# A fifth pair of rows in each quarter of the down projection, with the plain additions ahead of the joining ones

## The chip, the cores and the metric

The kernel is one program on one core of a Trainium2 chip. The metric is the device time of one execution in microseconds (us); several executions are timed and their median is given. The core has a matrix engine (PE, with its weight loads listed as PEld), a vector engine (DVE), a scalar engine (ACT), GpSimd (POOL) and a queue for transfers (SP). Each engine works through its own list of instructions in the order in which the program holds them; semaphores tie the lists together. A matrix product is written into one of eight banks of PSUM, each 128 x 512 floats.

## The reference, cut to what matters

One layer of a hybrid decoder runs on 256 tokens of width 2048: attention in two forms, gates, an output projection, a feed-forward part (up, a causal convolution of width 3, gelu times value, down), and an embedding gate (pg). The change touches the feed-forward part, above all `down`:

```python
up = causal_depthwise_conv(u @ w_up[i], conv_w[i], conv_b[i])
gate_ff, value = jnp.split(up, [D_FF], axis=-1)          # D_FF = 5632
f = (jax.nn.gelu(gate_ff, approximate=True) * value) @ w_down[i]
h = h + rmsnorm(f, g_ffn_post[i])
```

All inputs are float32. A product is made from three matrix products of reduced operands: each factor x is split into a high part (rounded) and a low part (x minus the high part), and high x high, high x low and low x high are summed. "Three products" below means these.

## The kernel before, in words

**Rows and quarters.** The 5632 inner rows of `down` are 44 blocks of 128 ("rows" from here on), worked in four quarters of 11 rows (`NQ`, `QT`). A quarter first makes its 22 tiles of `up` (one per gate row and one per value row; `mm` at L382 and L384, then `up_evac`), and then multiplies its 11 rows with the 2048 columns of `w_down`, adding to the running sum `ff`. Of these columns, the first 1024 go through `strassen` and the last 1024 through two calls of `plain` (columns 1024 to 1535 and 1536 to 2047), which call `four`. In the first quarter (q = 0) `plain(2)` stands ahead of `strassen`; in the other three both plains stand behind it.

**Pairs and plain rows.** In `strassen` a pair of rows is a 2 x 2 block product (two halves of the tokens, two rows, two column groups of 512) made with seven products instead of eight: 7 x 3 = 21 matmuls of 128 x 512. A plain row takes 2 x 2 x 3 = 12, so two plain rows take 24. `DROWS = 8` gives four pairs and three plain rows (L1431: `range(DROWS, QT)`). A pair needs sums of four token blocks (`parts`, L1209 to L1212, split at L1215 and L1218 into `mixed`) and sums of weight blocks. Of the weight sums, the first two of a pair are made by transfers while `up` runs (`sum_early`: one load by SP, two adding transfers by POOL, into `tsum`); the next two are made by DVE from them (`wsum`, L257 and L258). `sum_early` is called at the places in `AHEAD` (L1394, L1401).

**Weights.** Weights come in items of 128 x 1024. SP loads an item into `raw` (five buffers, `NRAW`), ACT writes its high part (`hi`, L238 or L234), DVE its low part (`lo`, L301 or L295), into seven buffers (`NSPL`). A pair has four items (a row, two of sums, half a row), a plain row one, `plain(2)` five and a half. `tick` runs at the start of each item: it issues high parts ahead of their use, then the low parts (`lows`) of all items that had a high part before this tick, and the work handed over with `defer`. `lows` also issues the next loads; a `raw` buffer is loaded again when its low part is done.

**Where the sums go.** `strassen` takes eight banks: those of products 1, 5, 6 and 7, and one for each place (token half, column half) of the result, which collect products 2, 3, 4 and the plain rows. Product 1 is copied out by ACT (L1289). What is left for DVE is twelve additions of 128 x 512 in q > 0: eight in `join_to` (L1321 to L1328, from products 6, 7, 5) and four in `ends` (L1332, from the four places). Both are handed to `defer`, so they are issued in a later tick, behind that tick's low parts:

```python
bk = next(s)                                   # L1432, after the pairs
defer((None, ... join_to(o, bk, x)))           # L1434, q > 0
next(s)                                        # L1439, after the plain rows
defer((None, lambda bk=bk, o=o: ends(o, bk)))  # L1440
```

`plain(2)` then asks `bank()` for two banks (one for each token half); the pool gives banks whose last reader has been issued.

## Time and profile before

| what | value |
|---|---|
| median of 3 runs | 1431.91 us (1430.57 to 1432.77) |
| the profiled execution | 1429.95 us, of which 1428.2 us are the span of the profile |
| HBM traffic | 302.50 MB read, 215 GB/s over the span |
| DMA share of `up` of the second quarter (800 to 905 us) | 0.70 |
| DMA share of its `down` (911 to 967 us) | 0.66 |

The span runs from the first instruction to the last. A row of the timeline gives the start and length in us, the engine, the line, the operation, what it writes and reads, the shape, and how many equal instructions that follow each other were merged into it; in brackets stands how long the engine had been idle and what ended that. A matmul's end is modelled: the next one starts before it ends, so the distance from start to start says what a matmul takes.

### The profile page before, as it was taken

To read this page: it belongs to the slowest core of one execution; us is meant where nothing else is said; L and a number is where in the kernel's file an instruction comes from. 1 tells how busy PE (TensorE), PEld (TensorE's weight loads), DVE (VectorE), ACT (ScalarE), POOL (GpSimd) and SP (SyncE) were. 2 spreads that over 40 slices of the span, in tenths; PEclk is the share of its full clock that TensorE was granted. 3 is DMA by queue.
4 is the path that set the end of the run, shared out by engine and by line. 5 is a ranking of instruction groups with operands and counts; after the bars stand their busy time and mean duration, and the time that the engine had idled before them with its cause. 6 is when DMAs were issued, how large, how long until landed. Compare 5 with 4: busy or idle time off the path is not lost.

```text
span 1428.2 us, 20626 instructions
## 1 busy us (share of the span) xinstructions
PE 1421.1 (100%) x7511; PEld 1223.2 (86%) x7511; DVE 1156.9 (81%) x1777; ACT 858.1 (60%) x1296; POOL 53.4 (4%) x65
## 2 busy tenths in 40 slices
PE   9999999999999999999999999999999999999998
PEld 8888888888888888898888888888888888888787
DVE  7876666669889965689988788987889878898798
ACT  7665555566655655676666566645566455665564
POOL 0000000002110000000000000000000000000000
PEclk9999999999999999999999999999999999999999
DMA  7754746479985766558857785377853778538754
GB/s 290 268 169 157 246 145 220 149 235 254 300 230 198 268 217 221 192 175 267 253 168 245 243 264 179 109 271 233 263 183 111 266 229 266 187 113 321 210 177 162
DMA packets 93814, 309.10 MB, mean 216 GB/s; under 512 B 10256, under 2 KB 10896, under 8 KB 93456
## 3 DMA queue, kind: packets, MB, share of 16 engines
q1 hardware_dynamic: 85072, 292.05, 60.6%
q0 software_dynamic: 8640, 15.73, 6.4%
q8 instruction: 59, 0.97, 0.3%
q14 instruction: 43, 0.35, 0.1%
HBM read 302.50 MB, written 5.24 MB: 215 GB/s over the span
## 4 chain that ended last, share of the span: by engine, by line
PE 98%; DVE 1%; ACT 0%; issue 0%
PE mm L382 33%; PE mm L945 30%; PE mm L384 17%; PE mm L710 2%; PE mm L708 2%; PE mm L709 2%; PE mm L863 2%; PE mm L865 2%; PE mm L864 2%; PE S L382 0%; PE mm L404 0%; PE mm L403 0%; PE mm L402 0%; DVE lo L301 0%; PE S L721 0%; PE po L721 0%
## 5 line engine op out<-in xcount | busy, mean ns | idle before, releaser
L301 DVE TENSOR_TENSOR lo<-raw,hi 128x1024 fp32r<-128x1024 f32 (+1 forms) x498 | 581.3, 1185 | 115.0 <-ACT hi L238 110.2
L382 PE MATMUL mm<-u,hi 128*128 128x512 f32 x1804 | 627.4, 392 | 0.0
L238 ACT ACTIVATE hi<-raw 128x1024 fp32r<-128x1024 f32 (+1 forms) x498 | 504.1, 1026 | 189.9 <-PE mm L382 54.4
L384 PE MATMUL mm<-u,lo 128*128 128x256 f32 x1791 | 501.4, 280 | 0.0
L382 PEld LDWEIGHTS mm<-u,hi 128*128 128x128 f32 x1804 | 336.7, 187 | 72.4
L384 PEld LDWEIGHTS mm<-u,lo 128*128 128x128 f32 x1791 | 338.5, 189 | 0.6
L945 PE MATMUL mm<-hi,ft 128*128 128x512 f32 x544 | 173.4, 389 | 0.0
L945 PE MATMUL mm<-hi,u 128*128 128x512 f32 (+1 forms) x464 | 148.0, 389 | 0.6 <-DVE u L1503 0.5
L440 ACT ACTIVATE t<-mm 128x256 f32<-128x256 f32 x131 | 49.8, 380 | 149.3 <-PE mm L384 149.2
L945 PEld LDWEIGHTS mm<-hi,ft 128*128 128x128 f32 x544 | 102.1, 188 | 21.1
L945 PE MATMUL mm<-lo,ft 128*128 128x512 f32 x272 | 105.8, 389 | 0.0
L945 PEld LDWEIGHTS mm<-hi,u 128*128 128x128 f32 x464 | 86.4, 188 | 19.1 <-DVE u L1503 2.2
L443 DVE TENSOR_TENSOR s<-mm,t 128x256 f32<-128x256 f32 x116 | 49.0, 422 | 54.4 <-ACT t L440 54.4
L945 PE MATMUL mm<-lo,u 128*128 128x512 f32 (+1 forms) x232 | 89.6, 386 | 0.0
L382 PE MATMUL mm<-mg,hi 128*128 128x512 f32 x232 | 80.5, 392 | 0.0
L277 POOL DMA_DIRECT2D tsum<-in_w x36 | 31.7, 1017 | 886.4 <-DMA tsum<-in_w 269.1
L384 PE MATMUL mm<-mg,lo 128*128 128x256 f32 x230 | 64.4, 280 | 0.0
L234 ACT ACTIVATE hi<-wsum 128x512 fp32r<-128x512 f32 x68 | 41.2, 629 | 36.0 <-DVE wsum L257 27.1
L945 PEld LDWEIGHTS mm<-lo,ft 128*128 128x128 f32 x272 | 51.1, 188 | 10.5
L1232 ACT ACTIVATE cv<-cpad,cw 128x256 f32<-128x256 f32 x88 | 52.5, 596 | 11.7 <-DVE cpad L1227 11.6
L945 PE MATMUL mm<-hi,mixed 128*128 128x512 f32 x160 | 55.8, 389 | 0.0
L945 PEld LDWEIGHTS mm<-lo,u 128*128 128x128 f32 x232 | 43.6, 188 | 9.0 <-DVE lo L295 0.5
(327 smaller groups left out, 1871.2 us busy)
## 6 DMA issues: line engine op xcount, KB each, us to landing
raw<-in_w SPq DMA_DIRECT2D x470, 512.0 KB, 4.2
tsum<-in_w POOLq DMA_DIRECT2D x36, 256.0 KB, 6.9
raw<-in_w SPq DMA_DIRECT2D x32, 256.0 KB, 3.2
tsum<-in_w SPq DMA_DIRECT2D x13, 512.0 KB, 4.6
gh<-in_w SPq DMA_DIRECT2D x12, 512.0 KB, 5.9
gh<-in_w POOLq DMA_DIRECT2D x24, 256.0 KB, 7.7
hd<-in_head SPq DMA_DIRECT2D x6, 576.0 KB, 7.5
gh<-in_gx SPq DMA_DIRECT2D x6, 512.0 KB, 5.3
```

What stands on the lines that cost most here:

```text
L234: ACT.activation(hi[i][:, n * 512:(n + 1) * 512], x, AF.Copy)
L238: ACT.activation(hi[i][:, a:b], raw[i][:, a:b] if src is None else src, AF.Copy)
L277: nc.gpsimd.dma_start(x, w[stream[i] + 1 - NE][:, 512:], accum_op=OP.add)
L301: DVE.tensor_tensor(lo[i][:, a:b], raw[i][:, a:b] if src is None else src, f(hi[i][:, a:b]), OP.subtract)
L382: PE.matmul(ps, wh, rhs, start=first, stop=last, skip_group_check=True)
L384: PE.matmul(ps[:, :T], wl, rhs[:, :T], start=False, stop=last, skip_group_check=True)
L440: ACT.activation(t1[0], ps[:, T:], AF.Copy)
L443: DVE.tensor_tensor(out, ps[:, :T], t1[0], OP.add)
L708: PE.matmul(pv[t], xh, wh, start=kt == 0, stop=False)
L709: PE.matmul(pv[t], xh, wl, start=False, stop=False)
L945: PE.matmul(ps, x[i], w[j], start=first and n == 0, stop=last and n == 2, skip_group_check=True)
L1232: ACT.activation(y, c[:, 2:], AF.Identity, scale=cw[:, n, 2:3], bias=cw[:, n, 3:4])
```

## The change

The number of paired rows in a quarter of `down` goes from eight to ten: five pairs and one plain row. The fifth pair's mixed token sums get a tile of their own (`mixed4`, in the place of the `hx` tile with number 0), and its first two weight sums come by transfers in `up`, as those of the others do (`AHEAD` has a fifth place; the sum lies in the place of `hx` number 3). In q > 0, `ends` is now issued at once after the plain rows, and `join_to` after it, in two parts that `defer` hands to two ticks. In q = 0 the order is as it was.

```diff
 PAIRS = 4
-DROWS = 8
+DROWS = 10
 DSUM = {"down": DROWS // 2, "pg": 2}
...
-        tt(x2, bk[6], x, OP.add)
-        tt(o[0, 0], o[0, 0], x, OP.add)
-        tt(x, bk[7], x2, OP.add)
-        tt(x2, bk[5], x2, OP.subtract)
-        tt(o[1, 0], o[1, 0], x, OP.add)
-        tt(x, bk[5], x, OP.subtract)
-        tt(o[0, 1], o[0, 1], x2, OP.add)
-        tt(o[1, 1], o[1, 1], x, OP.add)
+
+        def banks_free():
+            tt(x2, bk[6], x, OP.add)
+            tt(o[0, 0], o[0, 0], x, OP.add)
+            tt(x, bk[7], x2, OP.add)
+            tt(x2, bk[5], x2, OP.subtract)
+
+        def rest():
+            tt(o[1, 0], o[1, 0], x, OP.add)
+            tt(x, bk[5], x, OP.subtract)
+            tt(o[0, 1], o[0, 1], x2, OP.add)
+            tt(o[1, 1], o[1, 1], x, OP.add)
+        defer((None, banks_free))
+        defer((None, rest))
...
         bk = next(s)
-        q == 0 and join_first(o, bk)
-        defer((None, (lambda bk=bk, o=o: join(o, bk)) if q == 0 else lambda bk=bk, o=o, x=x: join_to(o, bk, x)))
+        if q == 0:
+            join_first(o, bk)
+            defer((None, lambda bk=bk, o=o: join(o, bk)))
...
         next(s)
-        defer((None, lambda bk=bk, o=o: ends(o, bk)))
+        if q == 0:
+            defer((None, lambda bk=bk, o=o: ends(o, bk)))
+        else:
+            ends(o, bk)
+            join_to(o, bk, x)
```

What this does to the engines' lists shows best in the second quarter (q = 1); the third and fourth read alike.

**DVE, from the last pair's last item on, before.** `lo_9103` is the half row that ends the fourth pair, `lo_9116`, `lo_9128` and `lo_9137` are the three plain rows, and `lo_9150`, `lo_9162` and `lo_9174` the first three items of `plain(2)`; `mm_9026` is product 6.

```order
L301 TENSOR_TENSOR lo_9103<-raw_9001,hi_9102 128x512 [waits Activation_49]
L301 TENSOR_TENSOR lo_9116<-raw_9019,hi_9115 128x1024 [waits DMAHW7_49,Activation_49]
L301 TENSOR_TENSOR lo_9128<-raw_9059,hi_9127 128x1024 [waits DMAHW0_49,Activation_49]
L301 TENSOR_TENSOR lo_9137<-raw_9071,hi_9136 128x1024 [waits DMAHW1_49,Activation_49]
L301 TENSOR_TENSOR lo_9150<-raw_9107,hi_9149 128x1024 [waits DMAHW2_49,Activation_49]
L301 TENSOR_TENSOR lo_9162<-raw_9119,hi_9161 128x1024 [waits DMAHW3_49,Activation_49]
L301 TENSOR_TENSOR lo_9174<-raw_9131,hi_9173 128x1024 [waits DMAHW4_49,Activation_49]
L1321 TENSOR_TENSOR x2_9188<-mm_9026,x1_8971 128x512 [waits PE_49]
L1322 TENSOR_TENSOR ff_5993<-ff_5993,x1_8971 128x512
```

**The same place in the changed kernel.** `lo_9186` is the half row that ends the fifth pair, `lo_9199` the one plain row, `lo_9211` to `lo_9257` the first five items of `plain(2)`; `mm_9070`, `mm_9025`, `mm_9057` and `mm_9280` are the four places of the result, `mm_9025` that of the first token half and the second column group.

```order
L301 TENSOR_TENSOR lo_9186<-raw_9094,hi_9185 128x512 [waits Activation_49]
L301 TENSOR_TENSOR lo_9199<-raw_9106,hi_9198 128x1024 [waits DMAHW3_49,Activation_49]
L301 TENSOR_TENSOR lo_9211<-raw_9142,hi_9210 128x1024 [waits DMAHW4_49,Activation_49]
L301 TENSOR_TENSOR lo_9220<-raw_9154,hi_9219 128x1024 [waits DMAHW5_49,Activation_49]
L301 TENSOR_TENSOR lo_9233<-raw_9190,hi_9232 128x1024 [waits DMAHW6_49,Activation_49]
L301 TENSOR_TENSOR lo_9245<-raw_9202,hi_9244 128x1024 [waits DMAHW7_49,Activation_49]
L301 TENSOR_TENSOR lo_9257<-raw_9214,hi_9256 128x1024 [waits DMAHW0_49,Activation_49]
L1338 TENSOR_TENSOR ff_5993<-ff_5993,mm_9070 128x512 [waits PE_49]
L1338 TENSOR_TENSOR ff_5993<-ff_5993,mm_9025 128x512 [waits PE_49]
L1338 TENSOR_TENSOR ff_5993<-ff_5993,mm_9057 128x512 [waits PE_49]
L1338 TENSOR_TENSOR ff_5993<-ff_5993,mm_9280 128x512 [waits PE_49]
L301 TENSOR_TENSOR lo_9266<-raw_9223,hi_9265 128x1024 [waits DMAHW1_49,Activation_49]
```

The first addition stands behind six low parts of full items in both; what moved is that three of the six were plain rows before and one is now, that the additions are those of the four places, and that `join_to` (now L1323 to L1332) follows later.

**PE, from the last plain row into `plain(2)`, before.** `mm_9206` is a place of the result, `mm_9246` and `mm_9247` are the banks of `plain(2)` for the two token halves; in the built program `mm_9247` stands in bank 0, which `mm_9026` held.

```order
L945 MATMUL mm_9206<-hi_9136,ft_5994 128x512
L945 MATMUL mm_9206<-lo_9137,ft_5994 128x512
L945 MATMUL mm_9206<-hi_9136,ft_5994 128x512
L945 MATMUL mm_9246<-hi_9149,ft_5994 128x512 [waits Activation_49]
L945 MATMUL mm_9246<-lo_9150,ft_5994 128x512 [waits DVE_49]
L945 MATMUL mm_9246<-hi_9149,ft_5994 128x512
L945 MATMUL mm_9247<-hi_9149,ft_5994 128x512 [waits DVE_49]
L945 MATMUL mm_9247<-lo_9150,ft_5994 128x512
```

**The same place in the changed kernel.** `mm_9289` and `mm_9290` are the banks of `plain(2)`; `mm_9290` stands in bank 2, which `mm_9025` held.

```order
L945 MATMUL mm_9280<-hi_9198,ft_5994 128x512 [waits PE_49]
L945 MATMUL mm_9280<-lo_9199,ft_5994 128x512
L945 MATMUL mm_9280<-hi_9198,ft_5994 128x512
L945 MATMUL mm_9289<-hi_9210,ft_5994 128x512 [waits Activation_49]
L945 MATMUL mm_9289<-lo_9211,ft_5994 128x512 [waits DVE_49]
L945 MATMUL mm_9289<-hi_9210,ft_5994 128x512
L945 MATMUL mm_9290<-hi_9210,ft_5994 128x512 [waits DVE_49]
L945 MATMUL mm_9290<-lo_9211,ft_5994 128x512
```

The fourth matmul of `plain(2)` waited for the first addition of `join_to` (L1321, the last reader of `mm_9026`) and now waits for the second addition of `ends` (the last reader of `mm_9025`).

**DVE, near the end of `up` in the changed kernel.** `y4_8955` holds the fifth pair's token sums, `s_8960` is the sum of the next `up` tile, `lo_8949` the row item of the second pair.

```order
L483 TENSOR_TENSOR ft_5994<-cv0_8828,ft_5994 128x256 [waits Activation_49]
L1209 TENSOR_TENSOR y4_8955<-cv0_8709,cv0_8828 128x128
L1210 TENSOR_TENSOR y4_8955<-y4_8955,cv0_8709 128x128 [waits DVE_49]
L1211 TENSOR_TENSOR y4_8955<-cv0_8709 128x128
L1212 TENSOR_TENSOR y4_8955<-y4_8955,cv0_8828 128x128 [waits DVE_49]
L443 TENSOR_TENSOR s_8960<-mm_8884,t1_8946 128x256 [waits Activation_49]
L1227 TENSOR_TENSOR cpad_5995<-s_8960,R_76 128x256 [waits DVE_49]
L301 TENSOR_TENSOR lo_8949<-raw_8780,hi_8948 128x1024 [waits DMAHW3_49,Activation_49]
L1218 TENSOR_TENSOR mixed4_6181<-y4_8955,mixed4_6181 128x512 [waits Activation_49]
L1235 SCALAR_TENSOR_TENSOR cv0_8943<-cpad_5995,cw_77,cv0_8943 128x256 [waits Activation_49]
```

The five rows L1209 to L1212 and L1218 are new here; the others stood in the same order before.

## The prediction

> **What bounds the kernel now.** I read the page first (busy time, then the chain that ended last), then the waits of PE, then the busy time of each engine in the stretch of the second quarter's `down`.

> ```profile
> PE 1421.1 (100%) x7511; PEld 1223.2 (86%) x7511; DVE 1156.9 (81%) x1777; ACT 858.1 (60%) x1296; POOL 53.4 (4%) x65
> PE 98%; DVE 1%; ACT 0%; issue 0%
> PE z L594 <- DVE epsb L563: 1.1, 1, 1.1
> PE mm L945 <- DVE u L1503: 0.5, 2, 0.3
> PE mm L1492 <- DVE hx L1463: 0.3, 1, 0.3
> 911.00:967.00 56.00, 56.00 (x248) 46.37 (x247) 46.99 (x60) 31.57 (x39) 0.00 (x0) 1.00 0.66 223
> ```

> PE is the path: 98% of the chain, and its waits on other engines sum to 1.9 us, none of them in the four quarters. In the stretch from 911 to 967 us (second quarter's `down`; the columns are length, PE, PEld, DVE, ACT, POOL, granted clock, DMA share, GB/s) PE has no idle time and the clock is 1.00. So a matmul taken away is worth its full distance, and any new wait of PE costs its full length. DVE is second, 46.99 of 56 us there. The question is whether it stays second once the stage holds more of its work.

> **What is removed.** Two rows of PE's timeline, an item of twelve matmuls apart:

> ```profile
> 929.62 0.39 PE L945 MATMUL mm<-lo,ft 128*128 128x512 f32 x1
> 932.34 0.39 PE L945 MATMUL mm<-lo,ft 128*128 128x512 f32 x1
> 938.24 0.39 PE L945 MATMUL mm<-hi,ft 128*128 128x512 f32 x1
> ```

> 932.34 - 929.62 = 2.72 us for twelve, 0.227 us each. A quarter loses 24 matmuls and gains 21: 3 x 0.227 = 0.68 us, and four quarters save **2.72 us**. The third row is the first matmul of the second token half of `plain(2)`, the one that waits for a bank (found by asking for a window after the end of the matmul ahead). In the changed kernel PE would want to start it 0.68 us earlier, at 937.56.

> **What the fifth pair costs DVE.** DVE in the same quarter, from the third pair to the additions, with two rows of ACT and one of PE:

> ```profile
> 917.03 0.68 DVE L257 TENSOR_TENSOR wsum<-tsum,raw 128x512 f32<-128x512 f32 x1
> 922.51 0.68 DVE L257 TENSOR_TENSOR wsum<-tsum,raw 128x512 f32<-128x512 f32 x1
> 923.84 1.29 DVE L295 TENSOR_TENSOR lo<-tsum,hi 128x512 fp32r<-128x512 f32 x2
> 926.22 0.39 PE L945 MATMUL mm<-lo,mixed 128*128 128x512 f32 x1
> 926.25 5.22 DVE L301 TENSOR_TENSOR lo<-raw,hi 128x512 fp32r<-128x512 f32 x5
> 930.60 1.06 ACT L238 ACTIVATE hi<-raw 128x1024 fp32r<-128x1024 f32 x1 [1.22 <-DMA raw<-in_w]
> 931.70 1.23 DVE L301 TENSOR_TENSOR lo<-raw,hi 128x1024 fp32r<-128x1024 f32 x1 [0.23 <-ACT hi L238]
> 932.62 1.06 ACT L238 ACTIVATE hi<-raw 128x1024 fp32r<-128x1024 f32 x1 [0.96 <-DMA raw<-in_w]
> 933.71 1.23 DVE L301 TENSOR_TENSOR lo<-raw,hi 128x1024 fp32r<-128x1024 f32 x1 [0.79 <-ACT hi L238]
> 934.86 0.68 DVE L1321 TENSOR_TENSOR x<-mm,x 128x512 f32<-128x512 f32 x1
> 943.44 2.48 DVE L1332 TENSOR_TENSOR ff<-ff,mm 128x512 f32<-128x512 f32 x4
> DMA to landing us min/median/max: 3.5/4.5/4.8
> ```

> From the wsum of the third pair to that of the fourth DVE takes 922.51 - 917.03 = **5.48 us a pair** without idle time; PE takes 21 x 0.227 = 4.76. So DVE loses 0.72 us to PE in each pair. In the fourth pair it is still ahead: the low part of its first sums ends at 923.84 + 1.29 = 925.13, and PE reads it at 926.22, 1.1 us later. A fifth pair takes that to about 0.4.

> Behind the last pair's half row (the first of the five merged at 926.25) DVE does six low parts. The last two wait for ACT, and ACT for the transfer: the `raw` buffer of the sixth item is the one that the first of the six frees, at 926.25 + 0.60 + 1.22 = 928.1, and it lands 4.5 us later, at 932.6, which is the median of the view on `raw` for 926 to 940 us (last row). Only then, at **934.86**, comes the first addition. Now PE had three plain rows (8.16 us) to pass meanwhile, and the freed bank was there at 935.54, 2.7 us ahead of 938.24. In the changed kernel the same six low parts, with the same five buffers behind them, stand ahead of the first addition (the order above shows it), but PE passes one plain row, 2.72 us.

> **What else is put on DVE.** The fifth pair's token sums and their low part. The rows of the fourth pair, and the place where the fifth's will stand:

> ```profile
> 882.65 0.29 DVE L1209 TENSOR_TENSOR y<-cv,cv 128x128 f32<-128x128 f32 x1
> 883.58 0.42 DVE L443 TENSOR_TENSOR s<-mm,t 128x256 f32<-128x256 f32 x1
> 885.51 0.68 DVE L1218 TENSOR_TENSOR mixed<-y,mixed 128x512 fp32r<-128x512 f32 x1
> 886.12 0.48 DVE L1235 SCALAR_TENSOR_TENSOR cv<-cpad,cw,cv 128x256 f32<-128x256 f32 x1
> 903.88 0.42 DVE L483 TENSOR_TENSOR ft<-cv,ft 128x256 fp32r<-128x256 f32 x1
> 905.45 0.42 DVE L443 TENSOR_TENSOR s<-mm,t 128x256 f32<-128x256 f32 x1 [1.14 <-ACT t L440]
> ```

> The four sums take 883.58 - 882.65 = 0.93 us and fall into the 1.14 us for which DVE waits ahead of 905.45: nothing. The low part takes 886.12 - 885.51 = 0.61, call it **0.60**, and comes behind that wait; from there DVE's rows follow each other closely up to the additions (one wait of 0.49 at 915.89 hangs on DVE's own earlier result and moves along), so all of it arrives. Bounds: 0 if a wait takes it up, 0.77 if the sums spill over by the 0.17 us that they pushed L443 in the fourth pair's case.

> With it the fifth pair's sums come 1.1 - 0.72 - 0.60 = -0.2 us, that is 0.2 us late. This is no term of its own: PE would wait for the bank right after anyway.

> **The added wait.** First addition: 934.86 + 5.48 + 0.60 = 940.94. Four additions take 2.48 (last row but one above), so they start 0.60 apart and take 0.68: the second ends at 940.94 + 0.60 + 0.68 = 942.22. PE wants the bank at 937.56: a wait of **4.66 us**. The other two quarters with this order:

> ```profile
> 1114.27 0.68 DVE L1321 TENSOR_TENSOR x<-mm,x 128x512 f32<-128x512 f32 x1
> 1117.55 0.39 PE L945 MATMUL mm<-hi,ft 128*128 128x512 f32 x1
> 1293.82 0.68 DVE L1321 TENSOR_TENSOR x<-mm,x 128x512 f32<-128x512 f32 x1
> 1296.86 0.39 PE L945 MATMUL mm<-hi,ft 128*128 128x512 f32 x1
> ```

> Third: 1114.27 + 7.36 = 1121.63 against 1117.55 - 0.68 = 1116.87, 4.76 us. Fourth: 1293.82 + 7.36 = 1301.18 against 1296.18, 5.00. Sum **14.42 us**. Issuing `ends` ahead of `join_to` doesn't help here: both stand behind the same six low parts, and the bank now given is free after the second addition, where before it was free after the first. Queued behind the waiting matmul is the rest of `plain(2)`; for that wait ACT's high parts that need a buffer from PE, but five items are ready by then. DVE uses the wait for the additions, so nothing is late next.

> **The first quarter** keeps its order; product 6 is read by L1308 and the bank goes to the second plain there:

> ```profile
> 760.59 6.52 DVE L301 TENSOR_TENSOR lo<-raw,hi 128x512 fp32r<-128x512 f32 x6
> 767.03 0.68 DVE L1308 TENSOR_TENSOR ff<-mm,ff 128x512 f32<-128x512 f32 x1
> 773.88 0.39 PE L945 MATMUL mm<-hi,ft 128*128 128x512 f32 x1
> ```

> L1308 ends at 767.03 + 5.48 + 0.68 = 773.19; PE wants the bank at 773.88 - 0.68 = 773.20. The room of 6 us is used up to nothing. The token sums are made well ahead, so I take 0; up to 0.6 if they are not.

> **Edits at nothing.** The fifth pair's transfers in `up`: 1 MB more with the sums, 0.25 MB less of rows, a quarter; DMA is 0.70 busy in the `up` of the table, and the sums are asked for with nine of the 22 `up` tiles still to come; if that cover went, the fifth pair's sums would be late by what is missing. ACT's high parts, one and a half items of some 1 us and the token sums a quarter: ACT is busy 31.57 of 56. The later `join_to`: its banks are needed again after eleven items.

> **The sum.** -2.72 + 14.42 = +11.70. Against the profiled execution: 1429.95 + 11.70 = 1441.65. That execution lies 1.96 us below the median of the runs shown; from the median, 1431.91 + 11.70 = **1443.6 us**.

> **Bounds of this sum.** Low: the 0.60 is taken up, and the two waits for the transfer (0.23 + 0.79 = 1.02) vanish in each quarter: 14.42 - 3 x 1.62 = 9.56, hence +6.84, 1438.8. High: 0.17 more of token sums and a landing of 4.8 instead of 4.5 us in each, and 0.6 in the first quarter: 16.4, hence +13.7, 1445.6. So 1438 to 1446.5 with the runs' scatter.

> **Rivals.**
> - *The clock falls in the wait.* PE never idles for more than 1.1 us in this trace, and the granted clock is 1.00 in the stretch above; neither tells what a gap of 4.7 us does. If the clock fell to half for the length of one item after each gap, twelve matmuls would take 5.44 instead of 2.72 us: 3 x 2.72 = 8.2 more, 1451.8. For it: the gap is more than four times any that is seen. Against: no row shows any fall.
>   [...]
> - *No wait at all* (the other side). The place is DVE ahead of the second addition, and the point that decides is 937.56 (second quarter): if DVE were done there, by reaching it 4.66 us earlier, the 2.72 us would stand alone: 1429.2. Against it: the low parts in front take 6 x 1.14 = 6.8 us even without their waits, and start behind a fifth pair that DVE passes more slowly than PE. For it: only that DVE's order may leave more slack than one execution shows.
> - *Only the fifth pair is late.* The 0.2 us in three quarters without the wait for the bank: 1429.8. It needs the same early addition.

> **How the numbers follow.** Bank wait as summed: 0.68. With the falling clock: 0.17. Something longer still behind the wait: 0.05. The two without the wait: 0.10 together. The forecast is 1443.6; its own range is 1438 to 1446.5, and the range reaches up into the falling clock: 1438 to 1450. A measurement of this kernel can tell about 0.2% (2.9 us) from no change. The bank wait gives slower by 0.5% at its lower bound, so slower has 0.90; the 2.72 us alone are 0.19%, just inside, so of the 0.10 I give 0.06 to within and 0.04 to faster.

> **What would show it.** PE's waits would name L1338 three times with 4 to 5 us each, at the fourth matmul of `plain(2)`, and nothing of that kind in the first quarter. DVE's first L1338 would start some 6 us later against the start of the pairs than L1321 does now. The granted clock in `down` tells the first rival. It is wrong if PE shows no wait on L1338, if the waits are under 3 us, or if PE waits longer inside the fifth pair than behind it.

## The result and the profile after

| | before | changed |
|---|---|---|
| median of five runs | 1430.58 us | 1448.98 us |
| lowest and highest | 1430.33 and 1432.77 | 1445.50 and 1451.65 |
| the profiled execution, its span | 1429.95, 1428.2 | 1448.98, 1447.2 |
| matmuls on PE | 7511 | 7499 |

The ratio is 1.0123, with a 95% interval of 1.0106 to 1.0141: slower by 1.2%, 5.4 us above the forecast of 1443.6. That lies above the bounds of its sum (1446.5) and inside the wider range that reached up into the falling clock (1450). The changed kernel also scatters more: its five runs spread over 6.2 us, those of the kernel before over 2.4.

The busy time of PE and its share of the chain on the page, then PE's waits on other engines (line waited for: us in total, times, longest), then the row of the second quarter's `down`, all of the changed kernel:

```profile
PE 1425.9 (99%) x7499; PEld 1223.6 (85%) x7499; DVE 1175.1 (81%) x1821; ACT 867.4 (60%) x1316; POOL 60.5 (4%) x73
PE 91%; DVE 4%; issue 1%; ACT 1%; DMA 1%; ACTq 0%
...
PE mm L945 <- DVE ff L1338: 13.4, 3, 4.6
...
PE mm L384 <- DVE lo L301: 0.7, 1, 0.7
...
911.00:967.00 56.00, 51.80 (x220) 42.05 (x220) 48.13 (x65) 31.22 (x42) 0.00 (x0) 0.97 0.60 201
```

Before, PE was 98% of the chain; now it is 91%, and DVE holds 4%. The new wait on L1338 comes three times, 13.4 us in all. Beyond the 4.20 us that PE lacks in the stretch from 911 to 967 us, the granted clock there is 0.97, where it was 1.00. And PE is *busier* than before (1425.9 against 1421.1 us) with twelve matmuls fewer: its matmuls became slower somewhere. (The 0.7 us on L384 stands at 31 us, long before `down`. The repeat of the changed kernel below didn't show it, and the run of the new order alone did: scatter.)

DVE in the second quarter, then the three waiting matmuls on PE's timeline (start, length, idle time ahead and its releaser in brackets):

```profile
932.37 6.60 DVE L301 TENSOR_TENSOR lo<-raw,hi 128x512 fp32r<-128x512 f32 x6
939.75 1.23 DVE L301 TENSOR_TENSOR lo<-raw,hi 128x1024 fp32r<-128x1024 f32 x1 [0.78 <-ACT hi L238]
940.89 2.47 DVE L1338 TENSOR_TENSOR ff<-ff,mm 128x512 f32<-128x512 f32 x4
...
937.63 0.39 PE L945 MATMUL mm<-hi,ft 128*128 128x512 f32 x1
942.22 0.50 PE L945 MATMUL mm<-hi,ft 128*128 128x512 f32 x1 [4.20 <-DVE ff L1338]
...
1127.59 0.79 PE L945 MATMUL mm<-hi,ft 128*128 128x512 f32 x1 [4.58 <-DVE ff L1338]
...
1312.90 0.79 PE L945 MATMUL mm<-hi,ft 128*128 128x512 f32 x1 [4.60 <-DVE ff L1338]
```

The additions start at 940.89 (forecast 940.94), behind the half row and six low parts of full items. The matmul ahead of the waiting one starts at 937.63, so without the wait the next would have come at 937.63 + 0.227 = 937.86; it comes at 942.22, 4.36 us late. The profile's 4.20 counts from the modelled end of the matmul ahead, which lies 0.39 - 0.227 = 0.16 us behind its distance. Counted from distance to distance the three waits cost 4.36 + 4.74 + 4.76 = 13.9 us.

The clock is seen by cutting the time around the gaps into pieces of 3.41 us, at whose borders it changes in this trace (at 943.14, 946.55, 1127.46, 1130.87, 1311.78, 1318.60 and 1444.90 us; length, then PE, PEld, DVE, ACT and POOL with their counts, granted clock, DMA share, GB/s), with three rows of PE's timeline behind them:

```profile
936.31:939.72 3.41, 1.71 (x8) 1.09 (x6) 2.51 (x3) 2.12 (x2) 0.00 (x0) 1.00 0.91 326
939.72:943.14 3.42, 0.92 (x4) 0.79 (x5) 3.40 (x5) 2.11 (x2) 0.00 (x0) 1.00 1.01 387
943.14:946.55 3.41, 3.41 (x10) 2.62 (x9) 3.34 (x6) 0.83 (x1) 0.00 (x0) 0.50 0.69 225
946.55:949.96 3.41, 3.41 (x16) 2.80 (x16) 3.38 (x5) 1.25 (x2) 0.00 (x0) 1.00 0.50 137
...
1127.46:1130.87 3.41, 3.28 (x8) 2.60 (x9) 3.41 (x6) 0.12 (x1) 0.00 (x0) 0.50 0.66 238
...
1308.36:1311.78 3.42, 0.00 (x0) 0.00 (x0) 2.28 (x3) 2.41 (x3) 0.00 (x0) 1.00 0.97 358
1311.78:1315.19 3.41, 2.29 (x5) 1.82 (x6) 3.41 (x6) 1.93 (x2) 0.00 (x0) 0.50 1.03 425
1315.19:1318.60 3.41, 3.41 (x9) 2.64 (x8) 3.34 (x5) 1.06 (x1) 0.00 (x0) 0.50 1.00 398
...
943.35 0.63 PE L945 MATMUL mm<-lo,ft 128*128 128x512 f32 x1
943.78 1.05 PE L945 MATMUL mm<-hi,ft 128*128 128x512 f32 x2
944.63 0.63 PE L945 MATMUL mm<-lo,ft 128*128 128x512 f32 x1
```

After the gap the clock stands at 0.50 for one such piece in the second quarter, for one in the third and for two in the fourth. While it does, three matmuls take 944.63 - 943.35 = 1.28 us, 0.427 each instead of 0.227. A busy piece of 3.41 us at half clock thus loses 3.41 x (1 - 0.227 / 0.427) = 1.6 us. The four pieces hold 3.41 + 3.28 + 2.29 + 3.41 = 12.39 us of matmuls and so lose 5.8 us. So two things that the forecast kept apart, the wait and the falling clock, both happened.

### The profile page after: what moved, and what is told of

The parts are those of the page before. It is cut to its first block, busy times and chain, and to the rows that moved or that the text cites. A ratio compares the mean times of both kernels' runs of the same rounds, so it can differ in the third digit from the quotient of the medians.

```text
span 1447.2 us, 20686 instructions
## 1 busy us (share of the span) xinstructions
PE 1425.9 (99%) x7499; PEld 1223.6 (85%) x7499; DVE 1175.1 (81%) x1821; ACT 867.4 (60%) x1316; POOL 60.5 (4%) x73
## 4 chain that ended last, share of the span: by engine, by line
PE 91%; DVE 4%; issue 1%; ACT 1%; DMA 1%; ACTq 0%
PE mm L382 31%; PE mm L945 26%; PE mm L384 16%; PE mm L708 2%; PE mm L710 2%; PE mm L709 2%; PE mm L863 2%; PE mm L865 2%; PE mm L864 2%; DVE lo L301 1%; DVE lo L295 1%; DMA raw<-in_w 1%; ACT hi L238 1%; PE mm L404 0%; PE mm L403 0%
## 5 line engine op out<-in xcount | busy, mean ns | idle before, releaser
L301 DVE TENSOR_TENSOR lo<-raw,hi 128x1024 fp32r<-128x1024 f32 (+1 forms) x498 | 579.5, 1180 | 110.0 <-ACT hi L238 105.2
L238 ACT ACTIVATE hi<-raw 128x1024 fp32r<-128x1024 f32 (+1 forms) x498 | 502.1, 1022 | 188.2 <-PE mm L945 61.1
L384 PE MATMUL mm<-u,lo 128*128 128x256 f32 x1791 | 501.6, 280 | 0.7 <-DVE lo L301 0.7
L384 PEld LDWEIGHTS mm<-u,lo 128*128 128x128 f32 x1791 | 338.4, 189 | 1.8 <-DVE lo L301 1.0
L945 PE MATMUL mm<-hi,ft 128*128 128x512 f32 x504 | 167.7, 399 | 13.4 <-DVE ff L1338 13.4
L945 PE MATMUL mm<-hi,u 128*128 128x512 f32 (+1 forms) x464 | 147.9, 389 | 0.6 <-DVE u L1514 0.5
L440 ACT ACTIVATE t<-mm 128x256 f32<-128x256 f32 x131 | 49.8, 380 | 149.3 <-PE mm L384 149.2
L945 PEld LDWEIGHTS mm<-hi,ft 128*128 128x128 f32 x504 | 97.4, 193 | 35.7 <-DVE ff L1338 14.7
L945 PEld LDWEIGHTS mm<-hi,u 128*128 128x128 f32 x464 | 86.4, 188 | 19.1 <-DVE u L1514 2.2
L945 PE MATMUL mm<-lo,ft 128*128 128x512 f32 x252 | 100.7, 400 | 0.0
L443 DVE TENSOR_TENSOR s<-mm,t 128x256 f32<-128x256 f32 x116 | 48.9, 422 | 51.8 <-ACT t L440 51.8
L945 PE MATMUL mm<-lo,u 128*128 128x512 f32 (+1 forms) x232 | 89.6, 386 | 0.0
L277 POOL DMA_DIRECT2D tsum<-in_w x44 | 38.8, 1024 | 898.1 <-DMA tsum<-in_w 766.6
L234 ACT ACTIVATE hi<-wsum 128x512 fp32r<-128x512 f32 x76 | 46.3, 629 | 41.9 <-DVE wsum L257 35.1
L945 PE MATMUL mm<-hi,mixed 128*128 128x512 f32 x192 | 67.0, 389 | 0.0
L384 PE MATMUL mm<-mg,lo 128*128 128x256 f32 x230 | 64.4, 280 | 0.0
L945 PEld LDWEIGHTS mm<-lo,ft 128*128 128x128 f32 x252 | 48.8, 193 | 11.0 <-DVE lo L295 1.1
L945 PEld LDWEIGHTS mm<-lo,u 128*128 128x128 f32 x232 | 43.6, 188 | 9.0 <-DVE lo L295 0.5
```

What stands on the lines that cost most here:

```text
L234: ACT.activation(hi[i][:, n * 512:(n + 1) * 512], x, AF.Copy)
L238: ACT.activation(hi[i][:, a:b], raw[i][:, a:b] if src is None else src, AF.Copy)
L277: nc.gpsimd.dma_start(x, w[stream[i] + 1 - NE][:, 512:], accum_op=OP.add)
L301: DVE.tensor_tensor(lo[i][:, a:b], raw[i][:, a:b] if src is None else src, f(hi[i][:, a:b]), OP.subtract)
L384: PE.matmul(ps[:, :T], wl, rhs[:, :T], start=False, stop=last, skip_group_check=True)
L440: ACT.activation(t1[0], ps[:, T:], AF.Copy)
```

## The experiments

All runs are of kernels made from the changed one or from the one before by the few lines shown. The kernel before ran beside them with medians of 1430.3 to 1430.6 us, and each ratio is against it.

**One low part less ahead of the additions.** In the last three quarters the tick of the plain row no longer issues low parts as far as ACT has come, but only to the next item:

```diff
-            lows(max(before, min(i + 2, at["high"])))
+            lows(min(i + 2, at["high"]) if at["near"] else max(before, min(i + 2, at["high"])))
...
+        at["near"] = q > 0
         next(s)
+        at["near"] = False
```

> The changed kernel, but in the last three quarters the tick that issues the additions puts only two low parts ahead of them instead of six; all else is kept. Theory (the matmul waits for the bank that the second addition frees, and the additions stand behind the low parts): the first addition starts about 5 us earlier, no wait of PE on L1338 in any quarter, granted clock 1.00 in all of down, and what is left is the 12 saved matmuls, -2.7 us: about 1428 us, 20 us under the changed kernel. If the clock has its own cause, apart from the gap: the waits go, but the 6.8 us of half clock stay, about 1435. If it is DVE's total load that is too high: the low parts that come later make PE wait for them instead, 3 x 3 to 5 us, 1440 or more.

Measured: 1438.67 us, ratio 1.0055 (1.0041 to 1.0069). DVE's rows and PE's waits of this kernel, then pieces of 3.41 us as above:

```profile
932.89 5.22 DVE L301 TENSOR_TENSOR lo<-raw,hi 128x512 fp32r<-128x512 f32 x5
938.36 1.22 DVE L301 TENSOR_TENSOR lo<-raw,hi 128x1024 fp32r<-128x1024 f32 x1 [0.24 <-ACT hi L238]
939.50 2.47 DVE L1338 TENSOR_TENSOR ff<-ff,mm 128x512 f32<-128x512 f32 x4
...
PE mm L945 <- DVE ff L1338: 6.7, 3, 2.3
...
1120.30:1123.71 3.41, 1.51 (x7) 1.26 (x8) 3.41 (x6) 2.28 (x3) 0.00 (x0) 1.00 0.98 387
1123.71:1127.12 3.41, 3.41 (x10) 2.63 (x9) 3.38 (x5) 1.95 (x2) 0.00 (x0) 0.50 0.69 243
1301.20:1304.62 3.42, 1.77 (x8) 1.13 (x6) 3.21 (x5) 1.77 (x2) 0.00 (x0) 1.00 1.02 387
```

The expectation miscounted: five low parts of full items stand ahead of the additions, not two (behind the half row four full ones in the first row shown and one in the second). They are issued by the fifth pair's own ticks, which this edit doesn't touch. As a dose it is good all the same: one low part and its wait for ACT taken away, and each wait is 2.2 to 2.3 us instead of 4.2 to 4.6. No wait on L301 came, so DVE's total load isn't what fails. And of three gaps of 2.25, 2.20 and 2.26 us only the second was followed by half clock (the row from 1123.71 us).

**The fifth pair alone**, with the old order of the additions (`DROWS = 8` becomes 10 in the kernel before).

> The kernel before with ten rows in pairs instead of eight, and its old order of the additions (the joining ones first, the first of them frees the bank). Theory (the fifth pair takes away two of the three plain rows that covered the low parts): the wait is there in this order too, shorter by one addition, 4.3 - 0.6 = 3.7 to 4.1 us in each of three quarters, now on L1321; the clock falls after at least one of them; 1438 to 1447 us. If the new order of the additions made the wait: no wait on L1321, about 1428 us.

Measured: 1445.78 us, ratio 1.0106 (1.0092 to 1.0119). PE's wait, with the line of the old order:

```profile
PE mm L945 <- DVE x L1321: 10.4, 3, 3.6
```

The wait is there without the new order, 3.0 us less over three quarters, and half speed follows each of its three gaps of 3.60, 3.20 and 3.64 us: from 941.35, 1125.49 and 1309.99 us on three matmuls take 1.28 us (0.427 each). The mean granted clock of the execution is 0.995. So the fifth pair makes most of the wait, and the order adds 1.0 us to each (0.6 was expected; the other 0.4 wasn't traced).

**The new order alone** (`DROWS = 10` becomes 8 in the changed kernel).

> The changed kernel with eight rows in pairs, so that only the new order of the additions is left. Theory (the order alone costs 0.6 us of a cover of 2.7 us): no wait of PE on L1338, clock 1.00, the kernel before's time within 0.2%. If the order makes the wait: 3 waits of some 4 us, 1442 us or more.

Measured: 1434.01 us, ratio 1.0026 (1.0015 to 1.0037), just outside the 0.2%. DVE's rows in the second quarter, the matmul ahead of the waiting one and that one itself, and PE's waits on that line:

```profile
928.00 6.58 DVE L301 TENSOR_TENSOR lo<-raw,hi 128x512 fp32r<-128x512 f32 x6
935.55 2.47 DVE L301 TENSOR_TENSOR lo<-raw,hi 128x1024 fp32r<-128x1024 f32 x2 [0.96 <-ACT hi L238]
938.19 1.22 DVE L301 TENSOR_TENSOR lo<-raw,hi 128x1024 fp32r<-128x1024 f32 x1 [0.17 <-ACT hi L238]
939.33 2.47 DVE L1338 TENSOR_TENSOR ff<-ff,mm 128x512 f32<-128x512 f32 x4
...
939.77 0.39 PE L945 MATMUL mm<-hi,ft 128*128 128x512 f32 x1
940.66 0.50 PE L945 MATMUL mm<-hi,ft 128*128 128x512 f32 x1 [0.50 <-DVE ff L1338]
...
PE mm L945 <- DVE ff L1338: 1.7, 2, 1.2
```

"The order alone costs 0.6 us" was too cheap. With three plain rows, `ends` issued behind the last of them stands behind eight full low parts (5 + 2 + 1); the old first addition, deferred ahead of the plain rows, came to stand behind six. The additions start at 939.33, 4.5 us later than the old first one (934.86). But PE is late there too: it wants the bank at 939.77 + 0.227 = 940.00 where it was 938.24, 1.8 us later, of which 1.2 are waits at 31 and 461 us, long before `down`. Against PE the additions moved by 2.7 us, and it is the second of them that frees the bank, 0.6 later. The room of 2.7 us that the forecast had read there is overdrawn by 0.6; the matmul comes 0.66 late. Over its four quarters `down` became 2.4 us longer in this profile, so what the order costs here is about that; the rest of the 3.4 us lies outside it. In the changed kernel, with one plain row, both orders stand behind six, as the forecast said. The order is therefore a gain in neither kernel.

**Busy instead of idle.** The changed kernel with 36 matmuls of 256 columns that add zeros, right ahead of the waiting one:

```diff
+                    for _ in range(fill if t == 1 and k == 0 else 0):
+                        PE.matmul(ps[0][:, :256], ones, zero, start=False, stop=False, skip_group_check=True)
                     three_wide(ps[t], cut(src, k, t), got[k], k == 0)
...
-            four(("down", q, 4 * c), ps, ft, *((hold, 4) if last else ()))
+            four(("down", q, 4 * c), ps, ft, *((hold, 4) if last else ()), fill=36 if q and c == 2 else 0)
```

> The changed kernel with 36 added matmuls of 256 columns that add zeros, in the last three quarters right ahead of the matmul that waits, so that PE is busy for most of the wait (36 at 0.12 us if they go at half the distance of 512 columns, 4.3 us). If the idle gap is what lowers the clock: granted clock 1.00 throughout down, the waits on L1338 nearly gone and their time taken by the added matmuls, 6 to 7 us under the changed kernel: about 1442 us. If the clock falls for another reason (the same work at the same time, power): the half clock stays and the time is the changed kernel's, 1446 to 1450 us.

Measured: 1443.12 us, ratio 1.0091 (1.0077 to 1.0105). PE around the same matmul of this kernel (its lines are two higher), and its row for 900 to 1420 us; behind it the same row of the changed kernel:

```profile
936.85 4.47 PE L1360 MATMUL mm<-zero,ones 128*128 128x256 f32 x36
941.80 0.50 PE L947 MATMUL mm<-hi,ft 128*128 128x512 f32 x1 [0.49 <-DVE ff L1340]
...
900.00:1420.00 520.00, 517.94 (x2695) 441.57 (x2694) 447.45 (x703) 309.23 (x460) 21.15 (x24) 1.00 0.65 210
```

```profile
900.00:1420.00 520.00, 505.53 (x2566) 428.06 (x2565) 442.88 (x698) 305.55 (x457) 21.17 (x24) 0.99 0.65 207
```

The wait is the same wait, filled with work that is of no use, and the kernel is 1448.98 - 1443.12 = 5.9 us faster: the added work ends about where the wait ended, and what differs behind it is the clock. With PE busy in the wait the row shows 1.00 where the changed kernel has 0.99, so here it was PE's idleness that lowered the clock, at a price of 5 to 6 us: 5.9 by the medians, 5.8 by the four pieces at half clock above, 5.25 by the length of the last three quarters' `down` in the two profiles. 1443.1 is about the changed kernel without the fall of the clock; the forecast, which left it out, said 1443.6. That the two lie so close is in part luck, as the account below shows.

**The additions early.** The flag of the first experiment set from the last pair on (and ACT held to items whose transfer has been issued), so that two full low parts are ahead:

```diff
-        while at["high"] <= upto:
+        while at["high"] <= upto and (at["high"] in raw or at["high"] in sums):
...
             last = p == len(pairs) - 1
+            at["near"] = last and key[1] == "down" and key[2] > 0
```

> The changed kernel, but in the last three quarters DVE runs no further ahead than two items from the last pair on, so that only two full low parts (plain row, first item of the next product) stand ahead of the additions; the earlier attempt took one away of the low parts that stood there, and its wait fell from 4.4 to 2.4 us. Theory: additions from about 935.8 us in the second quarter, the second of them done about 937.1 to 937.5, where PE wants the bank at 937.6 to 937.8: no wait on L1338 or under 0.5 us each, clock 1.00 throughout, and what is left is -2.7 us of matmuls plus 0.2 to 0.5 us in each quarter: 1428 to 1431 us. Rival (the low parts were only moved, DVE has too much work there): PE waits for L301 behind the additions instead, 1436 us or more.

Measured: 1429.34 us, ratio 0.9993 (0.9984 to 1.0002). DVE's rows and the first of PE's waits:

```profile
932.47 2.95 DVE L301 TENSOR_TENSOR lo<-raw,hi 128x512 fp32r<-128x512 f32 x3
935.45 2.73 DVE L1339 TENSOR_TENSOR ff<-ff,mm 128x512 f32<-128x512 f32 x4
...
PE mm L1505 <- DVE hx L1476: 1.5, 2, 1.2
```

Now it is the half row and two full low parts; the additions start at 935.45, no wait on them is left, and the clock is 1.00 from 900 to 1420 us. That takes 19.6 us off the changed kernel, the whole loss (and about 1 us beyond it, which the interval doesn't tell from none), with the fifth pair and the new order kept. The rival (DVE has too much work there) falls in this form: the low parts that were put behind the additions made no wait on L301. What came instead is a wait of 1.2 us at the end of the last quarter.

**Early, and three items' first token halves first** (in `four`, the second half starts behind the first half of `lag` items):

```diff
-                for t in range(2):
-                    three_wide(ps[t], cut(src, k, t), got[k], k == 0)
+                three_wide(ps[0], cut(src, k, 0), got[k], k == 0)
+                if k >= lag - 1:
+                    for j in range(k + 1) if k == lag - 1 else [k]:
+                        three_wide(ps[1], cut(src, j, 1), got[j], j == 0)
```

> As the run with the early additions, and the next product does the first token half of three items before the second half of the first (nine matmuls ahead of the second bank instead of three, 1.36 us more cover). Theory: no wait on L1338 at all, clock 1.00, 1428 to 1430 us. Rival: 1436 us or more through waits for L301, as six more matmuls need their low parts earlier.

Measured: 1430.95 us, ratio 1.0004 (0.9995 to 1.0013). PE's new wait:

```profile
PE mm L945 <- DVE lo L301: 1.0, 3, 0.3
```

The rival's wait for low parts does come, at a fraction of its price: the cover wasn't needed any more, and asking for items earlier costs 0.3 us in each quarter. So first halves done ahead can be overdone.

**Six first halves first, additions where the change has them** (`lag=6`, nothing else).

> The changed kernel, additions where it has them, but the next product does the first token half of six items before the second half of the first: 18 matmuls ahead of the second bank instead of three, 15 x 0.227 = 3.4 us more cover. Theory: each wait falls from 4.4 to 4.8 us to about 1.0 to 1.4 us, too short to lower the clock, so 1.00 throughout, and -2.7 + 3.6 + 1 = about +2 us against the kernel before: 1431 to 1434 us. Rival (something behind the bank sets the time): 1440 us or more, with a wait on another line.

Measured: 1432.59 us, ratio 1.0013 (1.0005 to 1.0022). PE's wait:

```profile
PE mm L945 <- DVE ff L1338: 2.4, 2, 1.2
```

As forecast, the wait shrinks by the cover given (to 1.2 and 1.1 us; in the fourth quarter none is listed), the mean granted clock is 0.999, as in the kernel before, and the time follows (1431 to 1434 expected). Without touching DVE's order at all, 16.4 of the 18.4 us come back: bringing PE to the bank later serves as well as bringing the additions forward.

**The changed kernel once more**, for the clock.

> The changed kernel once more, for the clock. If whole idle windows of 3.41 us that stand at fixed places in time lower it, the number of half clock stretches differs from execution to execution and the time with it: between none (about 1442 us) and four (about 1449 us). If each gap lowers it for a fixed time, the same 13.6 us at half clock and 1448.5 to 1449.5 us again.

Measured: 1447.92 us in its one run. Three pieces of 3.41 us, from the first gap on:

```profile
937.29:940.71 3.42, 0.28 (x2) 0.00 (x0) 2.41 (x3) 2.11 (x2) 0.00 (x0) 1.00 1.00 381
940.71:944.12 3.41, 2.20 (x5) 1.83 (x6) 3.41 (x6) 1.06 (x1) 0.00 (x0) 0.50 0.91 364
944.12:947.53 3.41, 3.41 (x9) 2.67 (x9) 3.34 (x6) 1.06 (x1) 0.00 (x0) 0.50 0.47 155
```

Two pieces at half clock follow the first gap here, where the profile above had one behind it. The mean granted clock is 0.995 over 1446.1 us, 0.994 over 1447.2 in the profile above, so the time at half clock is 13.0 to 15.9 us here and 15.95 there (13.65 in the four pieces, 2.30 at the end). The sum is about as a fixed time for each gap would have it; the two pieces behind the first gap are not. In the profile above the borders stay in place through the execution: the falls at 943.14, 1127.46 and 1311.78 us lie 54 times 3.413 us apart.

**Shorter gaps, for the clock** (18 added matmuls of zeros instead of 36).

> The changed kernel with 18 of the added matmuls of 256 columns instead of 36 ahead of the matmul that waits: gaps of PE of about 2.3 us, three of them, for the clock. If what lowers it is a fixed window of 3.41 us that is idle for more than half (as the runs so far read: 1.89 us idle lowered it, 1.70 us didn't), a gap of 2.3 us lowers it where 1.7 to 1.9 us or more of it fall into one window and not otherwise: 0 to 3 falls, each to be told from the window's place. If a whole idle window is needed: none.

Measured: 1443.56 us in its one run, gaps of 2.31, 1.40 and 2.45 us, one fall. The piece ahead of the fall, and the emptiest one around the third gap:

```profile
939.77:943.19 3.42, 1.24 (x5) 1.05 (x6) 3.42 (x6) 1.96 (x2) 0.00 (x0) 1.00 0.99 386
...
1308.41:1311.82 3.41, 1.77 (x8) 1.45 (x9) 3.41 (x6) 2.44 (x3) 0.00 (x0) 1.00 1.04 377
```

The gap of 2.45 us did nothing and that of 2.31 us lowered the clock: 2.17 us of idle time lie in the one piece, 1.64 in the other. The mean granted clock of 0.999 over 1441.8 us leaves room for one such piece at half clock (at most 4.3 us). This is as expected of pieces at fixed places that are idle for more than half, and speaks against a whole idle piece being needed: the one with 1.24 us of matmuls was followed by half clock.

**Early in two quarters, six first halves in the last.** The flag from the last pair on in the second and third quarters; in the fourth, where it left the wait of 1.2 us, only the first experiment's flag, with `lag=6` (ACT is held as in the run with the early additions throughout):

```diff
-            at["near"] = last and key[1] == "down" and key[2] > 0
+            at["near"] = last and key[1] == "down" and 0 < key[2] < NQ - 1
...
-            four(("down", q, 4 * c), ps, ft, *((hold, 4) if last else ()))
+            four(("down", q, 4 * c), ps, ft, *((hold, 4) if last else ()), lag=6 if end and c == 2 else 1)
...
+        at["near"] = q > 0
         next(s)
```

> As the run with the early additions in the second and third quarters. In the fourth, where that left PE a wait of 1.2 us for DVE at the end of down, only one low part less ahead of the additions, and the next product does the first token half of six items before the second half of the first. Theory (the early additions hold back transfers, and the last quarter's end feels it): no wait on L1338 and none over 0.3 us at the end of down, clock 1.00, 1427.5 to 1428.8 us, 0.1 to 0.2% under the kernel before. Rival (the fifth pair's load on DVE reaches the end of down in any order): the wait of about 1.2 us at the end of down stays, 1429 to 1430 us.

Measured: 1428.69 us, ratio 0.9989 (0.9980 to 0.9998): faster than the kernel before, by 0.1%, the only one of these whose interval lies below 1, and the best of several that were tried. Chain and second quarter of this kernel:

```profile
PE 98%; DVE 1%; ACT 0%; issue 0%
...
911.00:967.00 56.00, 56.00 (x247) 46.09 (x246) 51.23 (x68) 33.32 (x43) 0.00 (x0) 1.00 0.66 225
```

PE is the path again, with no idle time in the stretch, though DVE is busy for 51.23 of 56 us there. The wait at the end of the last quarter is gone with the early additions of that quarter, which agrees with the theory that these hold back transfers. The traces show the late transfer: with the early additions ACT waits 2.43 us, until 1322.29, for one of the last items of `down`, and DVE's low part (from 1323.38) and its closing additions stand behind it; here ACT waits 0.68 us for the same item, until 1318.83. Why that transfer came late wasn't followed.

**The first flag and six first halves in all three quarters.**

> The changed kernel with one low part less ahead of the additions and six items' first token halves ahead of the second half, in all of the last three quarters: the wait of 2.4 us of the first attempt less 3.4 us of added cover. Theory: no wait on L1338, clock 1.00, 1427.5 to 1429 us. Rival: as before, a wait at the end of down of 1 us or more, or waits for L301: 1429 to 1432 us.

Measured: 1429.13 us, ratio 0.9993 (0.9985 to 1.0002). No wait on L1338, none on L301 and none over 0.3 us at the end of `down`. Its profile has a wait of 1.4 us at 462 us, in a stage that the edits don't touch. The two last kernels can't be told apart: their runs cover 1428.01 to 1430.33 and 1428.47 to 1431.17 us.

## Why the prediction came out as it did

The length of each quarter's `down`, from the start of its first matmul to the start of its last, shows where the time went (us, one profile each):

| kernel | first | second | third | fourth |
|---|---|---|---|---|
| before | 56.94 | 56.93 | 56.94 | 56.93 |
| changed | 56.41 | 62.62 | 62.91 | 64.03 |
| early in two quarters, six first halves in the last | 56.44 | 56.50 | 56.51 | 56.48 |

- **The matmuls removed** (-2.72): their count is as forecast (7499 against 7511), the gain was put too high. Where nothing waits for the bank, in the last row, the four quarters are 1.8 us shorter, not 2.72, and the medians of the last two kernels show 1.3 and 1.75. Most of what is lacking is the next point.
- **What the fifth pair costs DVE** (0.72 us against PE, 0.60 for its low part): as forecast. The additions started at 940.89 where 940.94 was worked out. In the pair itself PE reads its own low part a little late:

```profile
932.17 0.39 PE L945 MATMUL mm<-hi,ft 128*128 128x512 f32 x1
932.50 0.50 PE L945 MATMUL mm<-lo,ft 128*128 128x512 f32 x1
932.84 0.39 PE L945 MATMUL mm<-hi,ft 128*128 128x512 f32 x1
```

  Two distances of 0.33 and 0.34 instead of 0.227: 0.2 us late, the 0.2 of the forecast. As it said, that is no term of its own where the wait for the bank follows: PE wants the bank at 937.86 instead of 937.56, and the wait is shorter by as much. Where no wait follows, it comes off the gain.
- **The bank wait** (+14.42): it is there, at the fourth matmul of `plain(2)`, three times, on the line named; 13.9 us from distance to distance. The 0.56 us less aren't all time won: in each of the three quarters PE wants the bank 27.48 or 27.49 us after its `down` began, 0.44 earlier than before (27.92) and not 0.68. That is the fifth pair's lateness again, and in the fourth quarter it is the whole of the 0.24 (4.76 instead of 5.00).
- **The first quarter** (0): nearly as forecast. Its `down` begins 0.59 us later than before (731.59 against 731.00). L1308 starts at 773.07 and so ends at 773.75 (forecast 773.19 + 0.59 = 773.78), and the matmul that wants its bank starts at 773.81 (773.20 + 0.59 = 773.79). No wait is listed, but the matmul behind it comes 0.34 us later instead of 0.227, 0.1 us lost.
- **The term that was mis-sized is the clock.** The forecast's sum priced a gap of PE at its length, so the clock stood at 0 in it, and "no row shows any fall" was taken as an argument for 0.17. It measured 5 to 6 us. A trace that has no gap over 1.1 us ahead of PE's last matmul can't speak against a fall in one of 4.7 us. And the trace of the kernel before does show a fall, at its very end, where PE has run out of work:

```profile
1422.84:1426.25 3.41, 0.41 (x4) 0.20 (x2) 1.61 (x4) 0.66 (x2) 0.00 (x0) 1.00 0.11 39
1426.25:1428.20 1.95, 0.00 (x0) 0.00 (x0) 0.00 (x0) 0.00 (x0) 0.00 (x0) 0.50 0.19 67
```

  A piece with 0.41 us of matmuls was followed by half clock there: that the clock had fallen after 3 us without matmuls stood in the trace that the forecast was worked out from. The rival's own price, 8.2 us by one item of twelve matmuls at half clock behind each gap, was too high: in the changed kernel's profile it is 3.41 or 6.83 us of half clock, at 0.427 us a matmul instead of twice 0.227.
  In these runs the fall wasn't tied to a piece that is wholly idle: in the first experiment one in which PE was busy for 1.51 of 3.41 us was followed by half clock. All three gaps of 4.20 to 4.60 us in the changed kernel's profile, and all three of 3.20 to 3.64 us in that of the fifth pair alone, were followed by a fall.

From the forecast to the measurement: by the table `down` became 18.2 us longer, where the sum had 11.7. Of the 6.5 us between, 5.8 are the clock. About 0.1 us is lost behind each of the four places where PE stopped, since the next matmul comes some 0.33 us behind instead of 0.227 (0.33 at 942.22 us, 0.34 at 773.81). The last 0.3 weren't traced. The medians differ by 18.4 us (1448.98 - 1430.58), so `down` holds the loss. The forecast of 1443.6 was counted from 1431.91 for the kernel before, 1.3 us above its median here; this error and the 0.7 us that the sum lacked beside the clock work against each other, and that is the luck in its nearness to 1443.1.

## What to carry to other kernels

Rows that an optimisation takes off the bottleneck engine may have been the cover of a release further on: before moving them, look up which accumulator the next product takes over, who reads it last, and how many instructions stand ahead of that reader in its queue. Give such a reader its place by the time at which its buffer is wanted, not behind all work that happens to be ready; here that, and a few first halves done ahead, turned a loss of 18 us into a gain of 1.75 (0.02 to 0.2% by its interval). And price a gap of PE at more than its length where the clock may fall in it: here three gaps of 4.20 to 4.60 us cost 5 to 6 us beyond their length.
